# One sum of each seven-product group: from VectorE to an accumulating DMA

## The chip, the cores and the metric

The kernel runs on one core of one Trainium2 chip. The metric is the device time of one execution in microseconds; smaller is better. The engines that matter here are TensorE (PE in the rows), VectorE (DVE), ScalarE (ACT), GpSimd (POOL), SyncE (SP) and the 16 DMA engines that move data between DRAM and the on-chip memory (SBUF).

## The reference

A decoder trunk of two layers, 256 tokens, model width 2048, all in float32:

```python
h = h + mamba2_mixer(rmsnorm(h), ...)      # in_proj 2048 -> 10304, out_proj 4096 -> 2048
h = h + swiglu(rmsnorm(h), ...)            # 2048 -> 2 x 5632 -> 2048
k, v, cum = shared_kv(h, ...)
h = h + forgetting_attention(rmsnorm(h), k, v, cum, w_q, ..., w_o)
h = h + swiglu(rmsnorm(h), ...)
```

Nearly all of the time goes into products of the 256-token activations with the weights, such as

```python
def swiglu(h, w_gate_up, w_down):
    g, u = jnp.split(h @ w_gate_up, 2, axis=-1)
    return (jax.nn.silu(g) * u) @ w_down
```

## The kernel before

**Units and pieces.** Weights come from DRAM in units of 1 MB: 512 input rows (four tiles of 128) by 512 output columns, as a tile `wraw` of 128 partitions. Three `wraw` buffers exist (`RAW`), and the load of a unit, issued by SyncE in `load` (line 347), waits until the unit three places earlier has been read for the last time. TensorE takes float32 as a high and a low half: ScalarE casts a piece of 128 x 1024 to `whi` (`split_hi`, line 260), VectorE subtracts it from the raw weights to give `wlo` (`split_lo`, line 266). Four `whi` and four `wlo` buffers exist (`SPL`), so the halves run at most four pieces ahead of TensorE. Each pair of a weight tile and a token tile takes three matmuls (lines 506 to 508): high times high, low times high, high times low. A plain unit is two pieces of twelve matmuls.

**Groups of seven products.** In the output projections, the gate-up and the down projections, two column blocks are done as a pair (`pair`, line 320): a left and a right unit for each group of 512 input rows. For some input groups (38 pairs of units in all) the two units together form a `Group`: instead of eight block products it takes seven, named by letters, on sums of weights and sums of activations (`split_cross` and `cross_step`). The left unit holds b11 and b21 (its even and odd weight tiles), the right unit b12 and b22. The weights that the products need are

- d: b21, g: b11, f: b12
- a: b21 + b22, c: b12 + b22
- e: b12 + b21 + b22, b: b11 + b12 + b21 + b22

VectorE makes four sums per group in place (line 384), each 128 x 1024. A product is six matmuls (lines 425 to 427). The sums of activations are made earlier and are not touched by the change.

**Order.** Every engine runs its own queue in the order in which the program is written. `stream` (line 433) makes halves four pieces ahead of the product that it emits; in a group the pieces are the letters of `Cross.ORDER`, "dgacebf". When the last piece of a unit has been split, `load_to` issues the load that takes over its buffer: in a group after e for the left unit and after f for the right one (line 459). Other work (activations, norms, sums) is written in between by `Flow.pump`, which keeps an account of how far each engine is.

**GpSimd** has little to do: a few powers (line 526) and twelve DMAs in the first layer and in the attention.

Of the kernel before, what the change touches and what calls it, by code (L numbers as in the profile page):

```python
# [12 lines left out]
ALU = mybir.AluOpType  # L13
# [21 lines left out]
KT = 4  # L35
# [4 lines left out]
RAW = 3  # L40
# [46 lines left out]
class Task:  # L87


    def __init__(self, gen, queue, ready=0.0):  # L90
        self.gen, self.queue, self.ready = gen, queue, ready
        self.done, self.evac, self.sync, self.on, self.last = False, False, False, None, "E"


class Flow:
# [7 lines left out]
    def spawn(self, gen, queue=None):  # L103
        q = self.urgent if queue is None else queue
        t = Task(gen, q, max(self.at["E"], self.current.ready if self.current else 0.0))
        q.append(t)
        return t
# [72 lines left out]
class Unit:  # L180


    def __init__(self, blk, kg, src, width, pieces):
        self.blk, self.kg, self.src, self.width, self.pieces = blk, kg, src, width, pieces
        self.raw = None


class Block:
# [8 lines left out]
class Cross:  # L197
# [5 lines left out]

    ORDER = "dgacebf"

    def __init__(self, left, right, parts):
        self.left, self.right, self.parts, self.ps = left, right, parts, {}
# [10 lines left out]
def kernel(ctx: ExitStack, tc: tile.TileContext, xT_d, x_d, cols_d, rows_d, wdt_d, win_d,  # L220
                     wout_d, gu0_d, dn0_d, wq_d, wk_d, wf_d, wv_d, wo_d, gu1_d, dn1_d, out_d):
    nc = tc.nc
# [15 lines left out]
    def nm(s):  # L238
        uid[0] += 1
        return f"{s}_{uid[0]}"  # L240
# [4 lines left out]
    def bank(shape):  # L245
        return mis.tile(shape, F32, tag="mis", name=nm("mis"))
# [11 lines left out]
    def split_hi(hi, src, scal=None):  # L258
        if scal is None:
            nc.scalar.copy(out=hi, in_=src)  # L260
        else:
            nc.scalar.activation(hi, src, AF.Copy, scale=scal)  # L262

    def split_lo(hi, lo, src, scal=None):
        if scal is None:
            nc.vector.tensor_tensor(out=lo, in0=src, in1=hi.bitcast(F32), op=ALU.subtract)  # L266
        else:
            nc.vector.scalar_tensor_tensor(out=lo, in0=src, scalar=scal, in1=hi.bitcast(F32),  # L268
                                           op0=ALU.mult, op1=ALU.subtract)
# [50 lines left out]
    def pair(xs, sources, done, fills, crossed, parts):  # L320


        both = [Block(xs, d, f) for d, f in zip(done, fills)]
        x = Cross(*both, parts)
        order, rights = [], []
        for kg in range(len(xs)):
            us = [Unit(b, kg, src[kg].rearrange("p (k n) -> p k n", n=NB), NB, [[0, 1], [2, 3]])
                  for b, src in zip(both, sources)]
            if kg in crossed:
                order += rights  # L330
                rights = []
                order.append(Group(x, us, xs[kg], kg == crossed[0], kg == crossed[-1]))
            else:
                for b, u in zip(both, us):
                    b.units.append(u)
                order.append(us[0])
                rights.append(us[1])
        blocks.append(order + rights)

    def slot_of(s):  # L340
        t = None
        while t is not s.task:
            t = s.task
            flow.finish(t)
        return s.tile

    def load(u, apart=False, before=None):
        n = sum(len(p) for p in u.pieces)
        u.raw = wraw.tile([P, n, u.width], F32, tag="wraw", name=nm("wraw"))
        for ks in u.pieces if apart else [range(n)]:  # L350
            if before is not None:
                before(ks)
            nc.sync.dma_start(out=u.raw[:, ks[0]:ks[-1] + 1, :], in_=u.src[:, ks[0]:ks[-1] + 1, :])

    def split_piece(u, ks):
        n = len(ks)
        us = n * u.width / 1024
        ready = flow.work("V", 1.14 * us, flow.work("A", 0.95 * us, flow.at["E"]) + LAT)
        raw = u.raw[:, ks[0]:ks[0] + n, :]
        wcol = u.blk.wcol  # L360
        if u.width < NB:
            both = wspl.tile([P, n, 2, u.width], F32R, tag="whi", name=nm("whi"))
            if wcol is not None:
                nc.vector.tensor_tensor(out=raw, in0=raw, op=ALU.mult,
                                        in1=cols[:, wcol + ks[0]:wcol + ks[0] + n].unsqueeze(2).to_broadcast([P, n, u.width]))
            split(both[:, :, 0, :], both[:, :, 1, :], raw)
            return both, None, ready
        hi = wspl.tile([P, n, u.width], F32R, tag="whi", name=nm("whi"))
        lo = wspl.tile([P, n, u.width], F32R, tag="wlo", name=nm("wlo"))
        if wcol is None:  # L370
            split(hi, lo, raw)
        else:
            for i, k in enumerate(ks):
                split(hi[:, i, :], lo[:, i, :], raw[:, i, :], col(wcol + u.kg * KT + k))
        return hi, lo, ready

    def split_cross(x, name):

        (g, u) = (v.raw.rearrange("p (j i) n -> p i j n", i=2) for v in x.units)
        b11, b21, b12, b22 = g[:, 0], g[:, 1], u[:, 0], u[:, 1]  # L380

        def add(out, in0, in1):
            flow.work("V", 1.22, flow.at["E"])
            nc.vector.tensor_tensor(out=out, in0=in0, in1=in1, op=ALU.add)  # L384

        src = {"d": b21, "g": b11, "a": b21, "c": b22, "e": b21, "b": b22, "f": b12}[name]
        hi = wspl.tile([P, 2, NB], F32R, tag="whi", name=nm("whi"))
        lo = wspl.tile([P, 2, NB], F32R, tag="wlo", name=nm("wlo"))
        split_hi(hi, src)
        if name == "g":  # L390
            add(b22, b12, b22)
        if name == "c":
            add(b21, b12, b21)
        split_lo(hi, lo, src)
        ready = flow.work("V", 1.22, flow.work("A", 1.05, flow.at["E"]) + LAT)
        if name == "d":
            add(b21, b21, b22)
        if name == "c":
            add(b22, b11, b21)
        return hi, lo, ready  # L400

    def cross_step(group, name, parts):

        hi, lo, ready = parts
        flow.work("E", 0.0, ready)
        x, act = group.cross, group.x
        s = slot_of(act)
        if act.adder is not None:
            flow.finish(act.adder)
        own = {"g": x.left.ps[0], "b": x.left.ps[1], "f": x.right.ps[0]}  # L410
        if group.first:
            if name == "d":
                flow.finish_all(False)
            x.ps[name] = own[name] if name in own else bank([P, NB])
        ps = x.ps[name]

        def a_of(part, p):
            if name in "dgb":
                k, t = {"d": (1, 0), "g": (0, 0), "b": (0, 1)}[name]
                return s[:, part, 2 * p + k, t * P:(t + 1) * P]  # L420
            return act.sums[:, "acef".index(name), part, p, :]

        for p in range(2):
            xh, xl = a_of(0, p), a_of(1, p)
            nc.tensor.matmul(ps, lhsT=xh, rhs=hi[:, p, :], start=group.first and p == 0 and name not in own, stop=False)  # L425
            nc.tensor.matmul(ps, lhsT=xh, rhs=lo[:, p, :], start=False, stop=False)  # L426
            nc.tensor.matmul(ps, lhsT=xl, rhs=hi[:, p, :], start=False, stop=group.last and p == 1 and name not in own)  # L427
        if group.last and name == "e":
            spawn(x.parts(x))
        flow.work("E", STEP)  # L430
        flow.pump()

    def stream(pre_load, pre_split):
        pieces, units = [], []
        for b in blocks:
            for u in b.units if isinstance(b, Block) else b:
                if isinstance(u, Group):
                    pieces += [(u, n) for n in Cross.ORDER]
                    units += u.units
# [6 lines left out]
        def load_to(n):  # L446
            while loaded[0] < min(n, len(units)):
                i = loaded[0]
                if i in pre_load:
                    pre_load[i]()  # L450
                load(units[i], i < 2, load_x0 if i == 0 else None)
                loaded[0] += 1

        def split_to(n):
            for i in range(len(parts), min(n, len(pieces))):
                u, ks = pieces[i]
                if isinstance(u, Group):
                    parts[i] = split_cross(u, ks)
                    if ks in "ef":
                        load_to(units.index(u.units["ef".index(ks)]) + 1 + RAW)  # L460
                    continue
                if i in pre_split:
                    pre_split[i]()
                parts[i] = split_piece(u, ks)
                if ks is u.pieces[-1]:
                    load_to(units.index(u) + 1 + RAW)
# [4 lines left out]
        for i, (u, ks) in enumerate(pieces):  # L471
            split_to(i + SPL)
            if isinstance(u, Group):
                cross_step(u, ks, parts[i])
                continue
            b = u.blk
# [844 lines left out]
```

## Time and profile before

| | |
|---|---|
| median of three runs | 2517.35 us (2516.65 to 2519.01) |
| the profiled execution | 2517.21 us, of which the span is 2515.4 us |
| TensorE busy | 2502.9 us (100% of the span) |
| VectorE busy | 1938.8 us (77%) |
| ScalarE busy | 1370.1 us (54%) |
| GpSimd busy | 39.5 us (2%) |
| share of the chain that ended last | PE 96%, DVE 3%, DMA 1% |
| granted clock of TensorE | 1.000 |
| DMA | 481.11 MB, mean 191 GB/s |

Busy times overlap, since the engines work side by side; what sets the time is the engine that the chain names. Starts in the rows below are counted from the start of the span.

### The profile page before, as it was taken

The numbers are of one execution on the slowest core, as the hardware profiler recorded it, in microseconds if no ns is written. First come the engines' busy times: TensorE is split into PE (matmuls) and PEld (weight loads), VectorE is DVE, ScalarE is ACT, GpSimd is POOL, SyncE is SP. The second block draws the span as 40 slices with busy tenths as digits, with TensorE's granted clock in tenths as the row PEclk, the third lists the DMA queues.
The fourth block names the chain that finished last, engine by engine and source line by source line (L and its number), as shares of the span: only waits on it lengthen the run. The fifth ranks groups of instructions, "written<-read, shape, count | busy, mean of one in ns | idle before, by whom it ended". The sixth has DMA issues, their size and how long they took to land.

```text
span 2515.4 us, 30043 instructions
## 1 busy us (share of the span) xinstructions
PE 2502.9 (100%) x11542; PEld 2076.0 (83%) x11542; DVE 1938.8 (77%) x2499; ACT 1370.1 (54%) x1733; POOL 39.5 (2%) x52
## 2 busy tenths in 40 slices
PE   9999999999999999999999999999999999999999
PEld 7888888887878888888888888888878888888887
DVE  7777777778788878788767667678887878879767
ACT  6665566555555555455545555655555555555544
POOL 0000000000000000000000000000000000000000
PEclk9999999999999999999999999999999999999999
DMA  7655455445554646465565555444555564645564
GB/s 269 223 175 174 178 182 203 167 168 196 186 203 168 218 167 223 178 217 184 181 216 187 200 175 203 163 168 170 182 182 203 184 215 169 219 167 206 200 230 150
DMA packets 68319, 481.11 MB, mean 191 GB/s; under 512 B 7600, under 2 KB 8256, under 8 KB 10576
## 3 DMA queue, kind: packets, MB, share of 16 engines
q1 hardware_dynamic: 66672, 468.64, 52.5%
q0 software_dynamic: 1504, 10.57, 1.0%
q8 instruction: 90, 1.47, 0.2%
q14 instruction: 53, 0.43, 0.0%
HBM read 477.00 MB, written 2.18 MB: 190 GB/s over the span
## 4 chain that ended last, share of the span: by engine, by line
PE 96%; DVE 3%; DMA 1%; ACT 0%; issue 0%; SPq 0%; ACTq 0%; DVEq 0%
PE acc L506 26%; PE acc L507 26%; PE acc L508 26%; PE mis L426 2%; PE mis L427 2%; PE mis L425 2%; PE acc L425 2%; PE acc L427 2%; PE acc L426 2%; PE mis L539 1%; DVE wlo L266 1%; PE mis L967 1%; DVE wraw L384 1%; PE mis L837 0%; DMA xraw<-in_xT_dram 0%; PE mis L973 0%
## 5 line engine op out<-in xcount | busy, mean ns | idle before, releaser
L266 DVE TENSOR_TENSOR wlo<-wraw,whi 128x1024 fp32r<-128x1024 f32 (+1 forms) x899 | 1079.7, 1220 | 349.1 <-ACT whi L260 341.2
L260 ACT CAST whi<-wraw 128x1024 fp32r<-128x1024 f32 (+1 forms) x902 | 929.4, 1049 | 740.4 <-PE acc L508 544.5
L506 PE MATMUL acc<-whi,xT 128*128 128x512 f32 x2816 | 1107.2, 393 | 0.5 <-ACT whi L260 0.4
L507 PE MATMUL acc<-wlo,xT 128*128 128x512 f32 x2816 | 1097.4, 390 | 1.0 <-DVE wlo L266 0.7
L508 PE MATMUL acc<-whi,xT 128*128 128x512 f32 x2816 | 1097.5, 390 | 0.0
L508 PEld LDWEIGHTS acc<-whi,xT 128*128 128x128 f32 x2816 | 528.9, 188 | 110.8
L507 PEld LDWEIGHTS acc<-wlo,xT 128*128 128x128 f32 x2816 | 529.4, 188 | 109.9 <-DVE wlo L266 2.6
L506 PEld LDWEIGHTS acc<-whi,xT 128*128 128x128 f32 x2816 | 529.3, 188 | 109.1 <-issue 1.2
L268 DVE SCALAR_TENSOR_TENSOR wlo<-wraw,cols,whi 128x512 fp32r<-128x512 f32 x192 | 134.6, 748 | 70.8 <-ACT whi L262 70.3
L262 ACT ACTIVATE whi<-wraw,cols 128x512 fp32r<-128x512 f32 x192 | 127.5, 717 | 72.2 <-PE acc L508 67.1
L384 DVE TENSOR_TENSOR wraw<-wraw,wraw 128x1024 f32<-128x1024 f32 x76 | 93.0, 1224 | 3.3 <-DMA wraw<-in_wout_dram 1.0
L384 DVE TENSOR_TENSOR wraw<-wraw 128x1024 f32<-128x1024 f32 x76 | 93.1, 1225 | 2.6
L426 PE MATMUL mis<-wlo,xS 128*128 128x512 f32 x228 | 89.5, 393 | 4.2 <-DVE wlo L266 4.2
L427 PE MATMUL mis<-whi,xS 128*128 128x512 f32 x228 | 88.7, 389 | 0.0
L425 PE MATMUL mis<-whi,xS 128*128 128x512 f32 x228 | 88.7, 389 | 0.0
L266 DVE TENSOR_TENSOR xT<-mis,xT 128x512 fp32r<-128x512 f32 x52 | 33.5, 686 | 37.2 <-ACT xT L260 37.2
L260 ACT CAST xT<-mis 128x512 fp32r<-128x512 f32 x52 | 27.9, 590 | 53.4 <-PE mis L539 53.4
L425 PE MATMUL acc<-whi,xT 128*128 128x512 f32 x144 | 56.1, 389 | 0.0
L427 PE MATMUL acc<-whi,xT 128*128 128x512 f32 x144 | 56.0, 389 | 0.0
L426 PE MATMUL acc<-wlo,xT 128*128 128x512 f32 x144 | 56.0, 389 | 0.0
L426 PEld LDWEIGHTS mis<-wlo,xS 128*128 128x128 f32 x228 | 42.8, 188 | 15.9 <-DVE wlo L266 7.3
L526 POOL TENSOR_TENSOR rs<-ms,mhalf 128x4 f32<-128x4 f32 (+1 forms) x27 | 30.2, 1119 | 1494.8 <-DVE ms L524 1494.5
(241 smaller groups left out, 1890.7 us busy)
## 6 DMA issues: line engine op xcount, KB each, us to landing
wraw<-in_gu_dram SPq DMA_DIRECT2D x176, 1024.0 KB, 4.9
wraw<-in_dn_dram SPq DMA_DIRECT2D x88, 1024.0 KB, 4.9
wraw<-in_win_dram SPq DMA_DIRECT2D x78, 1024.0 KB, 4.9
wraw<-in_wout_dram SPq DMA_DIRECT2D x32, 1024.0 KB, 5.0
wraw<-in_wq_dram SPq DMA_DIRECT2D x16, 1024.0 KB, 5.0
wraw<-in_wk_dram SPq DMA_DIRECT2D x16, 1024.0 KB, 4.9
wraw<-in_wv_dram SPq DMA_DIRECT2D x16, 1024.0 KB, 4.9
wraw<-in_wo_dram SPq DMA_DIRECT2D x16, 1024.0 KB, 4.9
```

The source lines that it names most:

```text
L260: nc.scalar.copy(out=hi, in_=src)
L262: nc.scalar.activation(hi, src, AF.Copy, scale=scal)
L266: nc.vector.tensor_tensor(out=lo, in0=src, in1=hi.bitcast(F32), op=ALU.subtract)
L268: nc.vector.scalar_tensor_tensor(out=lo, in0=src, scalar=scal, in1=hi.bitcast(F32), op0=ALU.mult, op1=ALU.subtract)
L384: nc.vector.tensor_tensor(out=out, in0=in0, in1=in1, op=ALU.add)
L425: nc.tensor.matmul(ps, lhsT=xh, rhs=hi[:, p, :], start=group.first and p == 0 and name not in own, stop=False)
L426: nc.tensor.matmul(ps, lhsT=xh, rhs=lo[:, p, :], start=False, stop=False)
L427: nc.tensor.matmul(ps, lhsT=xl, rhs=hi[:, p, :], start=False, stop=group.last and p == 1 and name not in own)
L506: nc.tensor.matmul(b.ps[t], lhsT=xh, rhs=hi[:, j, :], start=k == 0, stop=False)
L507: nc.tensor.matmul(b.ps[t], lhsT=xh, rhs=lo[:, j, :], start=False, stop=False)
L508: nc.tensor.matmul(b.ps[t], lhsT=xl, rhs=hi[:, j, :], start=False, stop=k == nk - 1)
L526: nc.gpsimd.tensor_tensor(out=r, in0=ms, in1=mhalf[:, :width], op=ALU.pow)
```

## The change

The sum b12 + b22 is no longer made by VectorE. Behind the load of a group's right unit, GpSimd issues a second DMA that reads b12 (512 KB, the even weight tiles) from DRAM once more and adds it to b22 in the buffer, where the load has put it. This DMA waits for the load's landing. With b12 + b22 in place of b22, the other sums are made from it: b21 + (b12 + b22) behind d (for e), that less b12 behind c (for a), and b11 added to it behind e (for b). Three VectorE operations are left, and the products come in the order "dgceabf". The left unit's buffer is now handed on after b, the right one's after f as before. The task that combines the products is started after the fifth product, as before; it is now a.

```diff
-        self.raw = None
+        self.raw, self.summed = None, False
...
-    ORDER = "dgacebf"
+    ORDER = "dgceabf"
...
             if kg in crossed:
+                us[1].summed = True
...
+        if u.summed:
+
+            nc.gpsimd.dma_start(out=u.raw[:, 1:KT:2, :], in_=u.src[:, 0:KT:2, :], accum_op=ALU.add)
...
-        def add(out, in0, in1):
+        def add(out, in0, in1, op=ALU.add):
             flow.work("V", 1.22, flow.at["E"])
-            nc.vector.tensor_tensor(out=out, in0=in0, in1=in1, op=ALU.add)
-
-        src = {"d": b21, "g": b11, "a": b21, "c": b22, "e": b21, "b": b22, "f": b12}[name]
+            nc.vector.tensor_tensor(out=out, in0=in0, in1=in1, op=op)
+
+        src = {"d": b21, "g": b11, "a": b22, "c": b22, "e": b21, "b": b21, "f": b12}[name]
...
-        if name == "g":
-            add(b22, b12, b22)
-        if name == "c":
-            add(b21, b12, b21)
         split_lo(hi, lo, src)
...
         if name == "c":
-            add(b22, b11, b21)
+            add(b22, b21, b12, ALU.subtract)
+        if name == "e":
+            add(b21, b11, b21)
...
-        if group.last and name == "e":
+        if group.last and name == "a":
             spawn(x.parts(x))
...
-                    if ks in "ef":
-                        load_to(units.index(u.units["ef".index(ks)]) + 1 + RAW)
+                    if ks in "bf":
+                        load_to(units.index(u.units["bf".index(ks)]) + 1 + RAW)
```

VectorE's queue in one group of the first layer's gate-up projection, before (`wraw_1232_7242` is the left unit, `wraw_1239_7282` the right one; the rows of line 384 are the sums):

```order
L266 TENSOR_TENSOR wlo_1251_7348<-wraw_1232_7242,whi_1250_7347 128x1024
L384 TENSOR_TENSOR wraw_1232_7242<-wraw_1232_7242,wraw_1239_7282 128x2x512
L384 TENSOR_TENSOR wraw_1239_7282<-wraw_1239_7282 128x2x512
L266 TENSOR_TENSOR wlo_1253_7365<-wraw_1232_7242,whi_1252_7364 128x1024
L266 TENSOR_TENSOR wlo_1255_7382<-wraw_1232_7242,whi_1254_7381 128x1024
L384 TENSOR_TENSOR wraw_1232_7242<-wraw_1239_7282,wraw_1232_7242 128x2x512
L266 TENSOR_TENSOR wlo_1257_7398<-wraw_1239_7282,whi_1256_7397 128x1024
L384 TENSOR_TENSOR wraw_1239_7282<-wraw_1232_7242 128x2x512
L266 TENSOR_TENSOR wlo_1260_7411<-wraw_1232_7242,whi_1259_7410 128x1024
L266 TENSOR_TENSOR wlo_1263_7423<-wraw_1239_7282,whi_1262_7422 128x1024
L266 TENSOR_TENSOR wlo_1266_7434<-wraw_1239_7282,whi_1265_7433 128x1024
```

The same group after the change (the sums are line 389 now):

```order
L266 TENSOR_TENSOR wlo_1251_7349<-wraw_1232_7242,whi_1250_7348 128x1024
L389 TENSOR_TENSOR wraw_1232_7242<-wraw_1232_7242,wraw_1239_7282 128x2x512
L266 TENSOR_TENSOR wlo_1253_7366<-wraw_1232_7242,whi_1252_7365 128x1024
L266 TENSOR_TENSOR wlo_1255_7382<-wraw_1239_7282,whi_1254_7381 128x1024
L389 TENSOR_TENSOR wraw_1239_7282<-wraw_1232_7242,wraw_1239_7282 128x2x512
L266 TENSOR_TENSOR wlo_1257_7399<-wraw_1232_7242,whi_1256_7398 128x1024
L389 TENSOR_TENSOR wraw_1232_7242<-wraw_1232_7242 128x2x512
L266 TENSOR_TENSOR wlo_1260_7411<-wraw_1239_7282,whi_1259_7410 128x1024
L266 TENSOR_TENSOR wlo_1262_7421<-wraw_1232_7242,whi_1261_7420 128x1024
L266 TENSOR_TENSOR wlo_1266_7434<-wraw_1239_7282,whi_1265_7433 128x1024
```

One sum is gone, the second one has moved from ahead of g's low half to behind c's, and the third from c to behind e's. The first of the three now reads the right unit after the DMA has added to it.

GpSimd's queue from the last power of the first layer's mixer to the first gate-up group, before:

```order
L919 DMA e_622_3935<-acT_d_113 128x2048
L526 TENSOR_TENSOR rs_663_4195<-ms_662_4193,mhalf_104 128x2
L526 TENSOR_TENSOR rs_686_4317<-ms_685_4315,mhalf_104 128x2
L526 TENSOR_TENSOR rs_707_4441<-ms_706_4439,mhalf_104 128x2
L526 TENSOR_TENSOR rs_950_5785<-ms_949_5783,mhalf_104 128x2
```

And after the change:

```order
L529 TENSOR_TENSOR rs_707_4441<-ms_706_4439,mhalf_104 128x2
L357 DMA wraw_720_4496<-in_wout_dram 128x2x512
L357 DMA wraw_757_4694<-in_wout_dram 128x2x512
L357 DMA wraw_839_5165<-in_wout_dram 128x2x512
L357 DMA wraw_869_5327<-in_wout_dram 128x2x512
L357 DMA wraw_924_5633<-in_gu0_dram 128x2x512
L529 TENSOR_TENSOR rs_948_5769<-ms_947_5767,mhalf_104 128x2
L357 DMA wraw_995_5994<-in_gu0_dram 128x2x512
```

The accumulating DMAs stand between the powers; the power of the second norm (`rs_948_5769`) is behind that of the first gate-up group.

## Rows read from the trace of the kernel before

**Rows 1.** The page's top: span, busy time of each engine.

```profile
span 2515.4 us, 30043 instructions
PE 2502.9 (100%) x11542; PEld 2076.0 (83%) x11542; DVE 1938.8 (77%) x2499; ACT 1370.1 (54%) x1733; POOL 39.5 (2%) x52
```

**Rows 2.** TensorE's waits: total us, times, longest.

```profile
PE mis L426 <- DVE wlo L266: 4.2, 6, 0.9
```

**Rows 3.** Line 384, the sums: durations in ns; VectorE idle before it.

```profile
L384 DVE TENSOR_TENSOR wraw<-wraw,wraw x76: 1217/1224/1226, 563.5 to 2491.0; 128x1024 f32<-128x1024 f32 x76
L384 DVE TENSOR_TENSOR wraw<-wraw x76: 1224/1226/1227, 564.8 to 2493.7; 128x1024 f32<-128x1024 f32 x76
...
  DMA wraw<-in_wout_dram: 1.0, 2
```

**Rows 4.** Timeline, VectorE, an ordinary group: start us, us, operation [idle before].

```profile
930.88 1.23 DVE L266 TENSOR_TENSOR wlo<-wraw,whi 128x1024 fp32r<-128x1024 f32 x1 [1.50 <-ACT whi L260]
932.14 1.22 DVE L384 TENSOR_TENSOR wraw<-wraw,wraw 128x1024 f32<-128x1024 f32 x1
933.40 1.23 DVE L384 TENSOR_TENSOR wraw<-wraw 128x1024 f32<-128x1024 f32 x1
934.54 1.22 DVE L266 TENSOR_TENSOR wlo<-wraw,whi 128x1024 fp32r<-128x1024 f32 x1
...
941.49 4.77 DVE L266 TENSOR_TENSOR wlo<-wraw,whi 128x1024 fp32r<-128x1024 f32 x4
```

**Rows 5.** Timeline, TensorE, the same group and behind it.

```profile
937.99 0.39 PE L426 MATMUL mis<-wlo,xT 128*128 128x512 f32 x1
...
943.43 0.39 PE L426 MATMUL mis<-wlo,xS 128*128 128x512 f32 x1
...
952.95 0.39 PE L507 MATMUL acc<-wlo,xT 128*128 128x512 f32 x1
```

**Rows 6.** Timeline, SyncE: the right unit's load, and the later one; its landing.

```profile
923.14 0.33 SPq L353 DMA_DIRECT2D wraw<-in_gu_dram  x1
wraw<-in_gu_dram SPq DMA_DIRECT2D x1, 1024.0 KB, 5.1
...
942.74 0.33 SPq L353 DMA_DIRECT2D wraw<-in_gu_dram  x1
```

**Rows 7.** Timeline, ScalarE, behind the same group.

```profile
947.83 2.01 ACT L260 CAST whi<-wraw 128x1024 fp32r<-128x1024 f32 x2 [1.77 <-DMA wraw<-in_gu_dram]
```

**Rows 8.** Timeline, VectorE and TensorE, the first group without slack.

```profile
585.16 1.23 DVE L384 TENSOR_TENSOR wraw<-wraw,wraw 128x1024 f32<-128x1024 f32 x1 [0.16 <-DMA wraw<-in_wout_dram]
...
594.05 0.39 PE L425 MATMUL mis<-whi,xS 128*128 128x512 f32 x1
594.77 0.50 PE L426 MATMUL mis<-wlo,xS 128*128 128x512 f32 x1 [0.33 <-DVE wlo L266]
```

**Rows 9.** Timeline, VectorE and TensorE, the second group without slack.

```profile
671.77 1.23 DVE L384 TENSOR_TENSOR wraw<-wraw,wraw 128x1024 f32<-128x1024 f32 x1 [0.80 <-DMA wraw<-in_wout_dram]
...
681.67 0.39 PE L426 MATMUL mis<-wlo,xS 128*128 128x512 f32 x1
```

**Rows 10.** Timeline, SyncE and VectorE, two of four groups with small slack.

```profile
1194.35 0.33 SPq L353 DMA_DIRECT2D wraw<-in_dn_dram  x1
1201.68 1.23 DVE L384 TENSOR_TENSOR wraw<-wraw,wraw 128x1024 f32<-128x1024 f32 x1
...
2299.75 0.33 SPq L353 DMA_DIRECT2D wraw<-in_dn_dram  x1
2307.08 1.23 DVE L384 TENSOR_TENSOR wraw<-wraw,wraw 128x1024 f32<-128x1024 f32 x1
```

**Rows 11.** DMA issues: count, KB each, median us to landing (two at single windows).

```profile
wraw<-in_dn_dram SPq DMA_DIRECT2D x88, 1024.0 KB, 4.9
e<-acT_d POOLq DMA_DIRECT2D x8, 1024.0 KB, 5.5
acT_d<-acT POOLq DMA_DIRECT2D x1, 64.0 KB, 2.1
...
e<-acT_d POOLq DMA_DIRECT2D x1, 1024.0 KB, 4.6
...
e<-acT_d POOLq DMA_DIRECT2D x1, 1024.0 KB, 6.9
```

## Prediction

> **What bounds the kernel now.** I read the page's top first: TensorE is busy for 2502.9 of the 2515.4 us of the span [rows 1]. So the only time that any edit to the other engines can give back is what TensorE idles, about 12.5 us, and the start of the program holds part of that. The waits of TensorE come next: its largest, "mis L426 <- DVE wlo L266", is 4.2 us in six waits [rows 2], and L426 is the second matmul of a product of a seven-product group, the one that needs the low half made by VectorE. So in the groups VectorE is close behind TensorE, yet costs it next to nothing. The four adds of a group are the two rows of line 384, 76 of each, so 152 in 38 groups, 1.22 us each; VectorE waited for a load at the first of them in just two groups [rows 3].
>
> The rows of one ordinary group show how this works out. VectorE makes d's low half at 930.88, the first add at 932.14, the second at 933.40, g's low half at 934.54, and ends with e, b, f and one more at 941.49, back to back; a step of this queue is about 1.2 us [rows 4]. TensorE reads d's low half at 937.99 and that of the product in fifth place at 943.43 [rows 5], four products in 5.44 us, or 1.36 each. VectorE needs about two steps where TensorE needs one product. It starts the group 7 us ahead and ends it a bit under 1 us ahead.
>
> **The change part by part.**
>
> **The removed add.** 38 adds of 1.22 us leave VectorE, 46 us of its queue. On the path this is worth at most the stalls that VectorE causes in groups, 4.2 us [rows 2], since elsewhere TensorE never waits for it there. These six waits lie in four groups. In the new order e's add still stands between e's and a's low half, so the fourth and fifth products are still served 2.4 us apart against 1.36 of TensorE; I take 2.0 us of the 4.2 as won.
>
> **The added DMA and its wait.** The first add of a group now reads the sum that the DMA makes, so VectorE waits at that add, and ScalarE at c's high half, until the accumulating DMA has landed. Call the time from the landing of the right unit's load to that landing the lag. Behind the waiting add stand g's, c's, e's, a's, b's and f's low halves and everything else on VectorE; TensorE waits for those.
>
> How much lag is free in an ordinary group: the right unit's load is issued at 923.14 and takes 5.1 us [rows 6], so it lands at 928.2, and the first add starts 3.9 us later [rows 4]. From the first add to the end of a's low half, now in fifth place, are seven steps: add, g, c, subtraction, e, add, a, so 8.4 us. That half is needed at 943.43 [rows 5], so the add may start as late as 935.0, and a lag of 6.8 us costs nothing. In short, the free lag is the slack ahead of the first add plus 2.9 us; the saved add pays part of it. Read in the same way, 32 of the 38 groups have a slack of 3.1 to 5.8 us, so 6.0 us or more is free in them.
>
> Two groups have no slack. In the first (input group 6 of the output projection, column blocks 0 and 1) the add at 585.16 itself waited for the load [rows 8]. The fifth product's low half was due at 594.28, one matmul after 594.05, so the add would have to start by 585.9 and only 0.8 us is free; before, this group lost 0.5 us at 594.77 [rows 8]. The second is the same place of blocks 2 and 3: landing and add at 671.7, fifth product at 681.67 [rows 9], so 1.6 us is free. Its right load is also the last of three that follow each other behind the preceding group, and the first of these goes into that group's left buffer, which is freed one step of 1.2 us later now; I add this 1.2 us there. In the first I add nothing, because the preceding group there ends about a step earlier.
>
> Four more groups have a slack of 1.4 to 2.6 us; two of them are shown: issue at 1194.35 and 2299.75 [rows 10], landing 4.9 us later (the median of these loads, rows 11), adds at 1201.68 and 2307.08 [rows 10]. Other VectorE work of 0.7 to 1.4 us stands inside two of them, which leaves a free lag of 3.8 to 4.4 us.
>
> **How long the lag is.** No accumulating DMA is in this trace. The nearest rows are the other transfers that GpSimd issues: 64 KB in 2.1 us, 1 MB in 4.6 us at the quickest, 5.5 in the median, 6.9 where loads of SyncE were in flight [rows 11]. A plain transfer of 512 KB lies between the first two, at 2.1 + 448/960 x 2.5 = 3.3 us. An accumulating one also has to fetch the 512 KB that it adds to, so it handles at least the bytes of the 1 MB row: 4.6 us, and I take this, plus 0.1 us for GpSimd to react. The ends are 3.3 and 7.0 us. GpSimd has no other work near a group except one power of 128x2 ahead of the first group's activation, and it does not wait for that DMA's landing, only for its trigger.
>
> The Trainium skill ("DMA: Bandwidth & Descriptors", section "Anatomy of one DMA — SWDGE (gpsimd) path") fits a GpSimd-issued DMA as about 2.0 us plus its bytes over 436 GB/s. By that, 512 KB would take 3.2 us, and the sum below would be 2520; but for 1 MB it gives 4.4 us, under every one of these rows. The skill ("Collectives: The Full Stack", section "The bandwidth ceiling: the fold count and why AG ≠ RS ≠ AR") says that a reducing DMA reads two sources per result and so runs at half the rate of a copy, which speaks for the larger value; no run here shows it.
>
> **The new order and the buffers.** The order d g c e a b f changes neither the number nor the length of TensorE's matmuls. The left unit's buffer is now read last by b's halves and not by e's, one or two steps later. Its next load was issued at 942.74 [rows 6], and ScalarE waited 1.77 us for it until 947.83 [rows 7]. One step later it starts at 949.1, and its low half, 2.3 us after that, is there at 951.4; TensorE reads it at 952.95 [rows 5]. So the wait grows by 1.2 us and costs nothing as long as the lag stays in bounds. The 19.9 MB more that the DMAs move are 4% of the page's traffic and fall where the DMA engines have room.
>
> **The sum** at a lag of 4.7 us. First tight group: 4.7 - 0.8 - 0.5 = 3.4. Second: 4.7 - 1.6 + 1.2 = 4.3. The four groups of small slack, free lag 3.8, 4.2, 4.4, 4.4: 0.9 + 0.5 + 0.3 + 0.3 = 2.0. The other 32: 0. Won: -2.0. Together +7.7 us. The profiled execution took 2517.21 us, of which 2515.4 is the span and 1.8 lies around it; the median of the three runs is 2517.35, so the two agree. 2517.2 + 7.7 gives 2525 us.
>
> **The rivals.**
>
> *The DMA is as quick as a plain one* (lag 3.3): 2.0 + 2.9 + 0 - 2.0 = +2.9, so 2520 us, no change that can be told. For it: the 512 KB are read while few other packets are on the engines. Against it: it must also read what it adds to. This is also where the skill's fit leads. It holds up to a lag of about 4.2 us (+5.0).
>
> *The DMA is slow* (lag of 6 us and more): the addition, or sharing the engines with the next load, which is issued 1 to 2 us after the right unit has landed, makes the lag outgrow the ordinary groups' reserve. At 7.0 us the tight ones cost 5.7 + 6.6, the four 11.2, ten groups of slack 3.1 to 3.6 about 7.5, the rest 2: +33, so 2550 us. Beyond that each further microsecond costs 38. For it: the row of 6.9. Against it: half of the 1 MB rows are at 5.5 or under.
>
> *VectorE's relief counts and the DMA hides* even in the tight groups, because their right loads land earlier in the new order: all 4.2 us won, perhaps another 1: 2512 us. Against it: those loads followed each other at the DMA engines' own pace.
>
> That the change does not do what it says I leave out: the order of the changed kernel shows 38 such DMAs on GpSimd's queue and three adds a group.
>
> **How the numbers follow.** The forecast (lag 4.2 to 6, 2522 to 2536 us) has 0.48, the quick DMA 0.30, the slow one 0.17, the relief 0.05. What a measurement of this kernel can tell from no change is about 0.2%, 5.0 us, so the bounds are 2512.3 and 2522.4. Slower: 0.48 + 0.17 = 0.65. Same: 0.30 and a little of the relief, 0.32. Faster: 0.03. The range reaches from 2515, below the quick DMA's time, to 2560, past the slow one at 7 us; left out are a lag beyond 7.3 us (about 0.1) and most of the relief.
>
> **What would show it.** Right: line 389 (the adds) 114 times instead of 152; 38 GpSimd DMAs of 512 KB with 4.3 to 6 us from issue to landing; VectorE's first add in a group waiting for that DMA, about 0.8 us in ordinary groups and 4 to 5 in the two tight ones; TensorE waiting for low halves only around 590, 680 and in the four groups named, some 10 us in all. Wrong: a landing after 3.5 us (then 2520), or TensorE waiting in every group (then 2550 and more), or waits of TensorE for the loads behind a group.

## The result

The changed kernel takes 2645.23 us (median of 2635.92 to 2647.29), the kernel before 2517.43 beside it: a ratio of 1.050, 95% interval 1.047 to 1.053. It is 128 us slower. The forecast was 2525 with a range to 2560, so the direction was right and the size far off.

The profiled execution took 2647.29 us, of which 2645.5 is the span. First the page of after: the span and the engines' busy times, which answer to [rows 1], the DMA queue of GpSimd, and the chain that ended last.

```profile
span 2645.5 us, 30239 instructions
...
PE 2541.2 (96%) x11542; PEld 2070.9 (78%) x11542; DVE 1885.0 (71%) x2461; ACT 1363.4 (52%) x1733; POOL 81.3 (3%) x90
...
q0 software_dynamic: 11840, 30.49, 5.5%
...
PE 56%; DMA 19%; DVE 18%; ACT 3%; issue 3%; SPq 0%; POOLq 0%; POOL 0%; DVEq 0%; ACTq 0%
```

VectorE is busy for 54 us less than in [rows 1], 46 of them the removed sums, and TensorE has the same 11542 matmuls. But TensorE's share of the chain has gone from 96% to 56%: the chain now goes through DMAs (19%) and VectorE (18%). Next TensorE's two largest waits and VectorE's waits at the sums (line, what it waited for: total us, times, longest).

```profile
PE acc L429 <- DVE wlo L266: 47.6, 35, 4.6
PE mis L429 <- DVE wlo L266: 43.6, 68, 1.4
...
DVE wraw L389 <- DMA wraw<-in_gu_dram: 133.3, 22, 7.9
DVE wraw L389 <- DMA wraw<-in_dn_dram: 49.2, 8, 7.1
DVE wraw L389 <- DMA wraw<-in_wout_dram: 19.7, 3, 6.7
```

The 4.2 us in six waits of [rows 2] have become 91 us in 103. L429 is what L426 was, the matmul that needs a low half. VectorE now waits for the accumulating DMA in nearly every group, 6 us at a time (133.3 over 22 in the gate-up projections), where [rows 3] had two short waits in all. From 540 us of the span on, where the first group is near, TensorE's late starts of matmuls (whatever a start lies over 0.23 us behind the one before) add up to 142 us, against 16.6 before; these 125 us are nearly all of the 130 that the span grew by. The DMAs (issue, KB each, median us from issue to landing):

```profile
wraw<-in_gu_dram SPq DMA_DIRECT2D x176, 1024.0 KB, 5.3
...
wraw<-in_gu_dram POOLq DMA_DIRECT2D x22, 512.0 KB, 8.8
...
wraw<-in_dn_dram POOLq DMA_DIRECT2D x10, 512.0 KB, 7.3
...
wraw<-in_wout_dram POOLq DMA_DIRECT2D x4, 512.0 KB, 6.3
...
wraw<-in_wo_dram POOLq DMA_DIRECT2D x2, 512.0 KB, 6.0
```

An accumulating DMA of 512 KB is slower than every transfer in [rows 11] when it goes to the gate-up units. One ordinary group shows why and at what price; it is the group of [rows 4] to [rows 6], 38 us later in the span. First the timeline of SyncE and GpSimd: the right unit's load, the accumulating DMA and the next load.

```profile
960.92 0.33 SPq L354 DMA_DIRECT2D wraw<-in_gu_dram  x1
...
966.67 1.09 POOL L357 DMA_DIRECT2D wraw<-in_gu_dram  x1 [44.98 <-DMA wraw<-in_gu_dram]
...
966.77 0.33 SPq L354 DMA_DIRECT2D wraw<-in_gu_dram  x1
```

The time from issue to landing of these three, in the same order, each from the DMA view of a window that holds it:

```profile
wraw<-in_gu_dram SPq DMA_DIRECT2D x1, 1024.0 KB, 4.8
...
wraw<-in_gu_dram POOLq DMA_DIRECT2D x1, 512.0 KB, 8.7
...
wraw<-in_gu_dram SPq DMA_DIRECT2D x1, 1024.0 KB, 6.1
```

The right unit lands at 965.7. GpSimd starts its DMA at 966.67, 0.95 us later, and 0.1 us after that SyncE issues the next load. GpSimd's instruction runs until 967.76, SyncE's only until 967.10. The load, twice as large, lands first, at 972.9; the accumulating DMA lands at 975.4. The lag is 9.6 us. VectorE and TensorE in this group (timeline, as in [rows 4] and [rows 5]):

```profile
975.45 1.23 DVE L389 TENSOR_TENSOR wraw<-wraw,wraw 128x1024 f32<-128x1024 f32 x1 [5.98 <-DMA wraw<-in_gu_dram]
976.59 2.35 DVE L266 TENSOR_TENSOR wlo<-wraw,whi 128x1024 fp32r<-128x1024 f32 x2
978.98 1.23 DVE L389 TENSOR_TENSOR wraw<-wraw,wraw 128x1024 f32<-128x1024 f32 x1
980.12 1.22 DVE L266 TENSOR_TENSOR wlo<-wraw,whi 128x1024 fp32r<-128x1024 f32 x1
981.38 1.23 DVE L389 TENSOR_TENSOR wraw<-wraw 128x1024 f32<-128x1024 f32 x1
982.52 4.76 DVE L266 TENSOR_TENSOR wlo<-wraw,whi 128x1024 fp32r<-128x1024 f32 x4
...
977.86 0.50 PE L429 MATMUL acc<-wlo,xT 128*128 128x512 f32 x1 [1.00 <-DVE wlo L266]
981.40 0.50 PE L429 MATMUL mis<-wlo,xS 128*128 128x512 f32 x1 [0.52 <-DVE wlo L266]
983.79 0.50 PE L429 MATMUL mis<-wlo,xS 128*128 128x512 f32 x1 [0.74 <-DVE wlo L266]
```

VectorE starts the first sum the moment the DMA lands and then works back to back. TensorE waits at g's low half (977.86), at e's (981.40) and at a's (983.79), each a step or two of VectorE behind a sum. Starts are some 3 us late in all, and most of the ordinary groups read like this one.

### The profile page after: what moved, and what is told of

It is laid out like the page before. It is cut to its first block, busy times and chain, and to the rows that moved or that the text cites. A ratio compares the mean times of both kernels' runs of the same rounds, so it can differ in the third digit from the quotient of the medians.

```text
span 2645.5 us, 30239 instructions
## 1 busy us (share of the span) xinstructions
PE 2541.2 (96%) x11542; PEld 2070.9 (78%) x11542; DVE 1885.0 (71%) x2461; ACT 1363.4 (52%) x1733; POOL 81.3 (3%) x90
## 4 chain that ended last, share of the span: by engine, by line
PE 56%; DMA 19%; DVE 18%; ACT 3%; issue 3%; SPq 0%; POOLq 0%; POOL 0%; DVEq 0%; ACTq 0%
PE acc L509 16%; PE acc L510 16%; PE acc L511 16%; DMA wraw<-in_gu_dram 12%; DVE wlo L266 11%; DVE wraw L389 5%; DMA wraw<-in_dn_dram 4%; ACT whi L260 3%; DMA wraw<-in_wout_dram 2%; PE mis L970 1%; PE mis L542 1%; PE acc L429 1%; PE acc L430 1%; PE acc L428 1%; PE mis L429 1%
## 5 line engine op out<-in xcount | busy, mean ns | idle before, releaser
L510 PEld LDWEIGHTS acc<-wlo,xT 128*128 128x128 f32 x2816 | 529.0, 188 | 112.8 <-DVE wlo L266 4.5
L389 DVE TENSOR_TENSOR wraw<-wraw,wraw 128x1024 f32<-128x1024 f32 x76 | 93.1, 1225 | 223.0 <-DMA wraw<-in_gu_dram 133.3
L429 PE MATMUL mis<-wlo,xS 128*128 128x512 f32 x228 | 99.7, 437 | 43.8 <-DVE wlo L266 43.6
L429 PEld LDWEIGHTS mis<-wlo,xS 128*128 128x128 f32 x228 | 44.2, 194 | 82.2 <-DVE wlo L266 74.9
L429 PE MATMUL acc<-wlo,xT 128*128 128x512 f32 x144 | 61.1, 425 | 47.3 <-DVE wlo L266 47.3
L428 PE MATMUL mis<-whi,xS 128*128 128x512 f32 x228 | 91.8, 403 | 0.0
L430 PE MATMUL mis<-whi,xS 128*128 128x512 f32 x228 | 91.5, 401 | 0.0
L429 PEld LDWEIGHTS acc<-wlo,xT 128*128 128x128 f32 x144 | 27.2, 189 | 66.9 <-DVE wlo L266 61.6
L357 POOL DMA_DIRECT2D wraw<-in_gu_dram x22 | 24.0, 1091 | 973.7 <-DMA wraw<-in_gu_dram 587.2
```

The lines of the kernel that those rows point to most:

```text
L389: nc.vector.tensor_tensor(out=out, in0=in0, in1=in1, op=op)
L510: nc.tensor.matmul(b.ps[t], lhsT=xh, rhs=lo[:, j, :], start=False, stop=False)
```

## The experiments

Three questions: is it the lag at all, what is the lag made of, and does the DMA cost anything beside its lag. Lags in this part are worked out for all DMAs of a trace, from the landing of the right unit's load to the landing of the GpSimd DMA; in the changed kernel the median of the 38 is 9.4 us (6.5 to 11.3).

| kernel | us, median | ratio to before (95%) | median lag |
|---|---|---|---|
| the change | 2645.2 | 1.050 (1.047 to 1.053) | 9.4 |
| new order, no DMA | 2518.6 | 1.0003 (0.9993 to 1.0013) | none |
| plain copy | 2557.6 | 1.0161 (1.0146 to 1.0176) | 6.75 |
| next load behind | 2559.2 | 1.0173 (1.0157 to 1.0189) | 6.5 |
| right unit first | 2533.2 | 1.0063 (1.0048 to 1.0078) | 8.6 |
| right first, 34 DMAs | 2522.8 | 1.0023 (1.0014 to 1.0032) | 8.8 |
| right first, no DMA | 2523.8 | 1.0025 (1.0016 to 1.0034) | none |
| four groups as before | 2518.2 | 1.0005 (0.9996 to 1.0015) | 8.75 |

**New order, no DMA.** All of the change but the DMA: the order dgceabf, the later hand-over of the left buffer, and b12 + b22 made by VectorE behind d.

```diff
-        if u.summed:
-
-            nc.gpsimd.dma_start(out=u.raw[:, 1:KT:2, :], in_=u.src[:, 0:KT:2, :], accum_op=ALU.add)
...
         if name == "d":
+            add(b22, b12, b22)
             add(b21, b21, b22)
```

> The changed kernel's order d g c e a b f and its later hand-over of the left buffer, but VectorE makes b12 + b22 (behind d's low half) and no accumulating DMA exists: four sums a group again. Theory 'lag' (TensorE waits because the accumulating DMA lands 9.4 us behind the right unit's load): all of the loss is gone, 2517 us, within 5 either way; TensorE's waits for low halves under 10 us. Rival 'order' (the new order and the buffer that is handed on later make the stalls): most of the loss stays, over 2600 us.

Measured 2518.55 us, not to be told from before. TensorE's wait in the groups is that of [rows 2] or less:

```profile
PE mis L427 <- DVE wlo L266: 3.1, 5, 0.7
```

So neither the order nor the hand-over of the buffers costs anything that can be told; the whole loss comes with the DMA.

**Plain copy.** The same DMA without its addition: it copies b12 over b22, so b22 is missing from the sums.

```diff
-            nc.gpsimd.dma_start(out=u.raw[:, 1:KT:2, :], in_=u.src[:, 0:KT:2, :], accum_op=ALU.add)
+            nc.gpsimd.dma_start(out=u.raw[:, 1:KT:2, :], in_=u.src[:, 0:KT:2, :])
```

> The DMA behind the right unit's load copies b12 over b22 and adds nothing (so b22 is left out of the sums); same issuer, bytes from DRAM, waits and order. Theory 'lag, in two parts' (the addition makes each 2 KB row take 178 ns and not 84, 1.5 us for the 16 rows of an engine; the next load of SyncE gets ahead of it, 3 us): the landing comes about 1.5 us earlier, 7.9 us behind the load, and with 38 us for each microsecond beyond 7 the time is about 2590 us (2570 to 2610); only if its first packets now come ahead of the next load's, the lag is about 4.5 us and the time about 2525. Rival 'the addition is slow' (nearly all of the lag above that of a plain transfer is the addition's): issue to landing about 4.5 us in every group, also where a load is issued beside it, and 2525 us.

Measured 2557.57 us, between the two expectations, so both missed: 88 of the 128 us go with the addition, and yet a copy still costs 40. The DMA view (as above) says why:

```profile
wraw<-in_gu_dram POOLq DMA_DIRECT2D x22, 512.0 KB, 6.2
...
wraw<-in_wout_dram POOLq DMA_DIRECT2D x4, 512.0 KB, 4.2
...
wraw<-in_wo_dram POOLq DMA_DIRECT2D x2, 512.0 KB, 4.0
```

Where no load of SyncE is issued just then (most units of the output projections), a copy lands 4.0 to 4.2 us after its issue. In the gate-up units, where the next load follows at once, it takes 6.2. The load gets ahead of a copy too, but costs it 2 us and not 3.

**Next load behind.** The accumulating DMA as in the change, but the load that follows it is issued by GpSimd, behind it on the same queue.

```diff
+    behind = [False]
...
-            nc.sync.dma_start(out=u.raw[:, ks[0]:ks[-1] + 1, :], in_=u.src[:, ks[0]:ks[-1] + 1, :])
+            queue = nc.gpsimd if behind[0] else nc.sync
+            queue.dma_start(out=u.raw[:, ks[0]:ks[-1] + 1, :], in_=u.src[:, ks[0]:ks[-1] + 1, :])
+        behind[0] = u.summed
```

> The changed kernel, but the one load that follows each accumulating DMA in the program is issued by GpSimd behind it, on the same queue, and so cannot get ahead. Theory 'lag, in two parts': first packets 2.5 us behind the right unit's landing in all groups, lag 6.5 us, time about 2545 us (2530 to 2560). Rival 'the addition is slow': lag stays at 9 us and over, 2640 us.

Measured 2559.2 us: 86 us come back, with no other edit than who issues the next load, and behind what; theory and measurement are 14 us apart, within the range, and the rival's 2640 is out. The DMA view's row of the gate-up units, then TensorE's waits, then, from VectorE's timeline, the first sum of the same ordinary group:

```profile
wraw<-in_gu_dram POOLq DMA_DIRECT2D x22, 512.0 KB, 5.8
```

```profile
PE mis L433 <- DVE wlo L266: 16.5, 28, 1.1
PE acc L433 <- DVE wlo L266: 10.8, 3, 4.9
```

```profile
952.42 1.22 DVE L393 TENSOR_TENSOR wraw<-wraw,wraw 128x1024 f32<-128x1024 f32 x1 [2.82 <-DMA wraw<-in_gu_dram]
```

The DMA takes 5.8 us in every kind of unit now, and the lag is 6.2 to 6.7 us in most groups. In fifteen groups, all of them of the gate-up projections, TensorE loses nothing at all: VectorE still waits 2.82 us at the first sum here, and no one waits for VectorE. What is left is in the two groups without slack, where g starts 4.6 and 5.1 us late, and in groups with less reserve.

The lag is then taken apart, each part by the kernel that lacks it. A plain copy with no load beside it has a lag of 4.65 us, of which 0.65 is GpSimd's reaction to the landing. The addition makes it 6.5, 1.85 more. The load that gets ahead makes it 9.4, 2.9 more. By the packets of the traces, the first one of an accumulating DMA moves 1.8 us after its issue where it is undisturbed and 4 to 5 us after where a load follows it by a few tenths.

The changed kernel shows the same within itself. In one gate-up group the load happens to come 1.33 us behind the start of GpSimd's instruction, when its 1.09 us are over, and the DMA lands after 5.9 us (timeline of GpSimd and SyncE, then the DMA's row):

```profile
1891.59 1.09 POOL L357 DMA_DIRECT2D wraw<-in_gu_dram  x1 [44.80 <-DVE xsum L573]
...
1892.92 0.33 SPq L354 DMA_DIRECT2D wraw<-in_gu_dram  x1
...
wraw<-in_gu_dram POOLq DMA_DIRECT2D x1, 512.0 KB, 5.9
```

In the three groups where the load comes 1.3 us or more behind that start, the DMA takes 5.9 to 6.6 us; where it comes between 0.55 us ahead and 1.07 behind, 8.1 to 10.5. With the plain copy, whose instruction takes 0.72 us, loads 0.1 to 0.53 us behind leave it at 6.0 us and more, loads from 0.65 on at 5.0 or less. So a load seems to get ahead when it is issued before GpSimd's instruction is through. This is read from the groups of these two kernels and was not tried by a run; in the kernels below one group of the second down projection goes against it (8.5 to 9.7 us with a load 1.2 to 2.1 us behind).

**Right unit first.** The DMA as in the change, but each group's right unit is loaded ahead of its left one, and f comes ahead of b. The lag then runs while the left unit is on its way.

```diff
-    ORDER = "dgceabf"
+    ORDER = "dgceafb"
...
-                    units += u.units
+                    units += u.units[::-1]
```

> The changed kernel, but a group's right unit is loaded ahead of its left one, and f (the last reader of the right unit) comes ahead of b, so that buffers come free in the order of the loads. The right unit lands about 5.4 us earlier against VectorE's queue. Theory 'lag': the DMA may still land 9 us behind its load, but the slack ahead of the first add is now about 9 us and VectorE doesn't wait in ordinary groups; only the two groups whose loads were late anyway still lose some 3 to 5 us each: about 2520 us (2513 to 2532). Rival 'order': no such gain, over 2600 us. A third reading, that the DMA's traffic itself slows the loads: some 10 to 40 us stay, spread over all groups.

Measured 2533.24 us, one microsecond over the expected range. The lag is nearly as bad as in the change (8.6), and yet 112 of the 128 us are gone: in an ordinary group the first sum is not due before 9.2 us behind the right unit's landing. VectorE's row for the ordinary group has no wait, that for the first group without slack has one:

```profile
943.96 1.22 DVE L389 TENSOR_TENSOR wraw<-wraw,wraw 128x1024 f32<-128x1024 f32 x1
...
591.86 1.23 DVE L389 TENSOR_TENSOR wraw<-wraw,wraw 128x1024 f32<-128x1024 f32 x1 [4.55 <-DMA wraw<-in_wout_dram]
```

So accumulating DMAs of slow landing are harmless where their time is covered. What is left sits mostly in three groups, with 10.8 of the 12.9 us for which TensorE still waits for low halves of groups.

**Right first, 34 DMAs.** As right unit first, but in the four groups of input group 6 VectorE makes the sum again.

```diff
-                us[1].summed = True
+                us[1].summed = kg != 6
...
         if name == "d":
+            if not x.units[1].summed:
+                add(b22, b12, b22)
```

> As the run with the right unit's load ahead of the left one's, and in addition the four groups whose first sum still waited for the accumulating DMA there (input group 6 of the output projection and of the second down projection, two column pairs each) get b12 + b22 from VectorE again; the other 34 keep the DMA. Theory (the whole loss is the lag between the right unit's landing and that of the accumulating DMA, where it outgrows the time that a group has free; the traffic and GpSimd's waits cost nothing): TensorE's waits for low halves of groups fall from about 13 us to under 5, and the time to 2516 us (2512 to 2520), no difference from the kernel before that can be told. Rival (part of what was left in that run is not the lag of those groups but 17 MB of added traffic or the clock, spread over the kernel): 2525 us or more.

Measured 2522.83 us, again between the two. Ten microseconds came back, six did not, and the timeline shows most of those at places that no longer have a DMA: TensorE waits 4.5 us in the two groups without slack. ScalarE and VectorE in the first group without slack:

```profile
584.72 2.00 ACT L260 CAST whi<-wraw 128x1024 fp32r<-128x1024 f32 x2 [3.63 <-DMA wraw<-in_wout_dram]
...
585.80 1.23 DVE L266 TENSOR_TENSOR wlo<-wraw,whi 128x1024 fp32r<-128x1024 f32 x1 [3.27 <-ACT whi L260]
```

Before, d's low half was done when the last of the two units landed, and a sum was the next thing [rows 8]. With the left unit loaded last, d itself waits for it, and VectorE does the sums from 586.9 on and not from 585.2. That accuses my new loading order and not the DMAs; two runs tell them apart.

**Right first, no DMA.** The kernel above without its 34 DMAs.

```diff
-                us[1].summed = kg != 6
+                us[1].summed = False
```

> As the run with the right unit first and 34 of the 38 DMAs, with none of them: VectorE makes all four sums in every group, the right unit is still loaded first and the products still come in the order dgceafb. The two kernels differ by the 34 DMAs and by 34 sums on VectorE. Theory (a DMA whose lag is covered costs nothing, the loss is the loading order's in the groups without slack): the same time as with the 34 DMAs, 2522 us (2520 to 2525). Rival (the traffic costs): that kernel's time less the DMAs' share, 2518 us or under.

**Four groups as before.** The kernel with right first and 34 DMAs, but the four groups of VectorE's sums load the left unit first.

```diff
-                    pieces += [(u, n) for n in Cross.ORDER]
-                    units += u.units[::-1]
+                    pieces += [(u, n) for n in (Cross.ORDER if u.units[1].summed else "dgceabf")]
+                    units += u.units[::-1] if u.units[1].summed else u.units
```

> As the run with the right unit first and 34 of the 38 DMAs, but the four groups whose sums VectorE makes also load their left unit first and take their products in the order dgceabf, so that in these groups only the place of one sum differs from the kernel before. Theory (what was left there came from the two groups without slack: their left unit, loaded last, reached ScalarE and VectorE too late, 3.2 and 2.3 us of TensorE's time; the 34 DMAs cost nothing): the time falls to 2518 us (2515 to 2520), within 0.2% of the kernel before, and TensorE's waits for low halves of the groups to 4 us or less. Rival (the 17 MB of added traffic or GpSimd's waits are what was left): 2521 us or more.

Without the DMAs the time is 2523.8 us, the same as with them; with the loading order put back in four groups it is 2518.2. TensorE's waits in the groups, first of the kernel without DMAs, then of the one with 34 and the old loading order in four groups:

```profile
PE mis L431 <- DVE wlo L266: 4.2, 7, 0.7
...
PE acc L431 <- DVE wlo L266: 1.3, 2, 0.9
```

```profile
PE mis L431 <- DVE wlo L266: 4.5, 7, 0.7
...
PE acc L431 <- DVE wlo L266: 0.9, 1, 0.9
```

The totals are alike, 5.5 and 5.4 us, and the two profiled executions (2520.8 and 2522.8 us) lie at the quick end of the eleven of the one kernel and at the slow end of the other, so they don't tell the 5.6 us between the medians. What they show is the place: in the two groups without slack TensorE waits 3.8 us in the first kernel and 1.4 in the second, whose other waits include 2.2 us in one of the last groups, where a lag of 10.5 us isn't covered.

The last kernel runs 34 accumulating DMAs with a median lag of 8.75 us and moves 18 MB more, and is as fast as the kernel before within what can be measured. With these two runs the rest is accounted for: the traffic costs nothing that can be told, and what was lost came from uncovered lags and, in the four groups, from the left unit loaded last. And they show the other half: VectorE is busy for 1895.3 us, 43 less than in [rows 1], and TensorE's waits for it in groups are still 5.4 us where [rows 2] had 4.2 and the new order without a DMA 3.1. The work taken off VectorE buys nothing measurable, even where the DMA is free. None of these kernels beats the one before.

## Why the prediction was wrong

**The step that failed is "How long the lag is".** It took 4.7 us with ends of 3.3 and 7.0; the median is 9.4. The mechanism of the forecast (the lag outgrows the reserve of a group) was right, and the term was mis-sized in each of its three parts:

- GpSimd's reaction was put at 0.1 us. It is 0.7 in the median, 0.95 in the group shown. No row of before showed a GpSimd DMA waiting for a load, so this was a guess without an upper end; the nearest, a DMA of GpSimd at 115.40 that waited for another one, started 0.3 us behind that one's landing.
- The DMA alone was taken to be as long as a 1 MB row, 4.6 us, since it handles that many bytes. It takes 5.8. Both steps to that figure were low: a plain copy of 512 KB takes 4.0 to 4.2 us and not 3.3, and the addition adds 1.7 and not 1.3.
- The load behind it was named among the rivals, as "sharing the engines", and given one end, the row of 6.9 us. The transfer of that row is no accumulating one, and sharing is not what the trace shows: the later load lands first, 2.5 us ahead in the group shown, and the first packet of the accumulating DMA moves when nine tenths of the load are already under way. This was worth 2.9 us of lag and 86 of the 128 us of time. The trace of before had a hint of it that the prediction left out: of the two 1 MB DMAs that GpSimd issues 0.6 us apart at 115.40, the first takes 6.9 us and the second, behind it, 8.8. The row of the two has their median:

```profile
e<-acT_d POOLq DMA_DIRECT2D x2, 1024.0 KB, 7.9
```

The Trainium skill's fit ("DMA: Bandwidth & Descriptors", section "Anatomy of one DMA — SWDGE (gpsimd) path"), 3.2 us for 512 KB, was further off than the row: the plain copy takes 4.0 to 4.2 here, the accumulating one 5.8. The Trainium skill ("Collectives: The Full Stack", section "The bandwidth ceiling: the fold count and why AG ≠ RS ≠ AR") tells of the steps of a ReduceScatter between cores that the add, with its two source reads, halves the rate of a copy. For this local DMA it points the right way. With the time before the first packet taken off, the data of the 512 KB took 2.6 us as a copy and 4.0 as an addition, in the runs with no load ahead: a factor of about 1.5. One packet of 2 KB takes 178 ns in the addition, and 84 among the plain transfers of the same trace.

**The free lag held.** Ordinary groups were given 6.8 us. With the next load behind, fifteen groups at lags of 6.2 to 6.7 lose nothing; with the plain copy, ordinary groups at lags of 6.9 to 7.6 lose 0.7 to 0.8 each.

**The price held at this lag, in part by luck.** The slow rival's sum was +33 us at 7.0 and 38 for each further microsecond: at 9.4 that is 33 + 91 = 124, so 2641, against 2645 measured. But some 8 us of the 128 come from a lower clock (below), which the sum doesn't have, and with the next load behind, at a lag of 6.5, the same working gives about 23 us where 42 were measured: 11.3 for the two groups without slack, 9.2 for the next four, about 2.5 for ten more. Two small slips change nothing: at a lag of 6 the terms of the forecast give 2533 us and not 2536, and the rival's +33 leaves out the 2.0 won. The rival's chance was 0.17 and the range stopped at 7.3 us of lag. So the range failed for the same reason as the forecast: an unknown that costs 38 us for each microsecond was bounded above by a row of a different kind of transfer.

**The groups without slack** were to cost 4.7 - 0.8 - 0.5 and 4.7 - 1.6 + 1.2; at the lag of 6.5 of the kernel with the next load behind, the same working gives 5.2 and 6.1, and g starts 4.6 and 5.1 late there. The size is right. Not foreseen: with the longest of these waits in the change the granted clock fell to half. The window table of after (us, busy time of PE, PEld, DVE, ACT and POOL, granted clock, DMA share, GB/s):

```profile
595.20:602.00 6.80, 5.95 (x14) 4.69 (x15) 6.68 (x7) 2.97 (x4) 0.00 (x0) 0.50 0.00 0
```

**The order, the buffers and the traffic** were costed at nothing, and rightly: the run without the DMA is 1.0003, and taking 34 DMAs out of a kernel that covers them changes nothing that can be told.

**The relief** of 2.0 us did not come. The new order alone, without a DMA, has 3.1 us of these waits against 4.2, a difference too small to tell in the time; with 34 DMAs and VectorE relieved they are 5.4, of which 2.2 belong to the one DMA that isn't covered.

Of the signs named, line 389 is there 114 times, as said. The landing was to be 4.3 to 6 us and is 8.6 in the median; the first sum was to wait 0.8 us in ordinary groups and waits 6; TensorE's waits were to be some 10 us and are 91, which is the sign given for "TensorE waiting in every group".

## What to carry to other kernels

An operation moved from a busy engine to a DMA trades its duration there for the time from trigger to landing, and the latter has to fit into the reserve of the place where it is first needed; ask for that reserve first, and take the operation off only where the engine it leaves was holding someone up. If the DMA waits for one load, look at what the other queues issue while its own instruction still runs, since the next load can land first although it is issued second. And where an unknown duration is multiplied by every group of a kernel, bound it by what has not been seen rather than by a row of something similar.

## What the chip showed that was not expected

- An addition by DMA (512 KB of float32, from DRAM into SBUF): 5.8 us alone and 8.8 in the median with a load behind it; a plain copy of the same bytes 4.0 to 4.2 and 6.2. GpSimd's instruction takes 1.09 us for the one and 0.72 for the other. VectorE makes the same sum in 1.22 us.
- A DMA of GpSimd whose instruction started 0.1 us ahead of a 1 MB load of SyncE landed 2.5 us behind it. The Trainium skill ("DMA: Bandwidth & Descriptors", section "SWDGE vs HWDGE vs iDMA") says that the queues of GpSimd and of SyncE are served in turn inside each DMA engine. By that the two should have moved in turn as soon as GpSimd's was ready, which without a load is 1.8 us after its issue. Here its first packet came 4 to 5 us after. Whether it was the data or the list of transfers that waited, these runs don't tell.
- The granted clock fell to half (the 1.2 GHz level of the two) in four places of the changed kernel, 17 us in all, each during a wait of TensorE of 1.9 to 4.6 us or within 1.4 us behind it; three other waits of 2.2 to 2.9 us (at 743, 839 and 1996) have no such fall. Matmuls that start every 0.23 us elsewhere start every 0.43 there. By an estimate from these two that is some 8 us of the 128. In the kernel before and in the new order without a DMA the clock doesn't fall until the last 1.5 us of the span.
